# Where the last query transposes are issued: ahead of the gates or between the gates' products

## The chip, the cores and the metric

One core of a Trainium2 chip runs the whole program in one launch. The metric is the device time of an execution in microseconds (us). The engines are TensorE (PE, with its weight loads as PEld), VectorE (DVE), ScalarE (ACT), GpSimd (POOL) and SyncE (SP, whose queue issues the DMAs); each works through a queue of its own in order, and semaphores hold an instruction until its inputs are there.

## What is computed

Two layers of a streaming encoder, for a prompt of 2048 tokens and 8 samples of 16 tokens, D = 1024, all float32. Layer 0 is an RMS norm, one wide projection, and two mixers whose outputs are gated, concatenated and projected back. Layer 1 is a pooled layer that this change doesn't touch.

```python
z = rms_norm(h, norm_g) @ w_in
a_q, a_k, a_v, a_g, b_qkv, b_g, b_beta, b_alpha = split_cols(z, AB_WIDTHS)
q = rms_norm(a_q.reshape(Bn, T, A_HEADS, A_HEAD_DIM), q_norm)
...
o_a = swa_prompt(q, k, v, sinks)             # mixer A: banded attention
o_a = o_a.reshape(Bn, T, A_WIDTH) * jax.nn.silu(a_g)
...
o_b, s_new = gated_delta_rule(bq, bk, bv, beta, g, s0.astype(f32), chunk)   # mixer B
o_b = rms_norm(o_b, o_norm).astype(h.dtype).reshape(Bn, T, B_WIDTH) * jax.nn.silu(b_g)
y = h + jnp.concatenate([o_a, o_b], axis=-1) @ w_out
```

## The kernel before, in words

The tokens are worked through in four groups of four 128-token blocks; group 0 also carries the samples as a fifth block (`GROUPS`, L31). A group runs all of layer 0 and then all of layer 1. Products are made in three passes of float32r (high times high, low times high, high times low): `proj_fm` (L695, products at L702 to L704) makes 128 output columns for up to 512 tokens (two pieces of 320 in group 0) with eight steps of three products; `tok_major` (L1273, products at L1281 to L1283) makes 256 columns for one block of 128 tokens.

Layer 0 treats the heads in two pairs. For each pair: the keys of mixer B (`b_keys`), then its queries and values (`b_queries`), each with a convolution; and the queries of mixer A (`a_queries`, L1359), ahead of `b_queries` for pair 0 and behind it for pair 1. After that come the gates: `gates_early(0)` (L1590), four projections whose results are multiplied at once into pair 0's outputs, and `gates(1)` (L1604), four more.

In `a_queries` each block's product is copied by ACT (L1376), squared by ACT and summed by DVE (`head_norm`, L1295 and L1296), raised to the power -1/2 by POOL (L501) and multiplied by POOL twice (L1304, L1305). Then four PE transposes (L1388; for the sample block two, L1383) bring it into columns; ACT copies them out (L1390) and DVE makes the low half (L1392). This last part is the job `qcols`. A job `end`, behind all blocks, frees two buffers and starts the attention of that pair, `a_attend` (L1425: scores at L1445 and L1446, softmax with DVE at L1449, transposes at L1459, products at L1474 to L1476; in group 0 also the samples' attention with two loads at L1535).

The order of the work is written by a small planner with a clock of its own, which counts estimated us. `tick(us)` is called after every step of products (0.64 for three products of 512 columns, 0.40 for 320, 0.64 for two steps of `tok_major`), advances the clock, issues the pending jobs that are due and lets the running jobs take their next steps. `defer(us, fn)` puts a job into `pend`; `start(gen)` starts a job that takes a step each time the planner's clock passes what its last step yielded; `queue` is worked off by one worker job in order; `drain()` (L396) steps that worker until the queue is empty; `flush()` (L377) issues all that is pending at once, whatever its due time; `finish(job)` (L368) steps a job to its end. The costs that matter here: `DEF` = 7.0 for `qcols` (7.1 for `end`), `ATT` = 2.4, 2.4, 1.2, 1.2 for the steps of an attention unit, `INV` = 0.6 for one of the 31 steps of mixer B's triangular inverse, `VAL` = 1.8 for a value job's wait.

```python
defer(DEF, qcols)            # L1395, for each block
...
def end():
    drop(*zs[0:2])
    st["A", jp] = start(a_attend(jp), 0.6)
defer(DEF + 0.1, end)
```

The planner's order is not the last word. What the program traces is put into the engines' queues by a builder that keeps this order as a priority, but takes an instruction that it reckons ready ahead of an earlier one that it reckons not ready. The trace shows it in places: gate products stand ahead of transposes that the code issues before them.

Mixer B of pair 1 runs beside the gates: `b_inverse` (L979) solves 32x32 blocks on DVE (L995, L996), copies the result (L1000), writes it to DRAM (L1002, L1003) and loads it back in another arrangement (L1011, L1013); PE then joins the blocks, beginning at L1022. The other loads on SP's queue are the weights: in group 0 from the input with a split into high and low (L459, L471, L475), later ready-made (L448), two ahead of use and three buffers in all; and the input rows of the residual (L1640).

Of the kernel before, what the change touches and what calls it, by code (L numbers as in the profile page):

```python
# [237 lines left out]
def hybrid_kernel(  # L238
# [24 lines left out]
    def buf(shape, tag, bufs=2, dt=F32):  # L263
        return sb.tile(shape, dt, tag=tag, name=nm(tag), bufs=bufs)
# [103 lines left out]
    def finish(*js):  # L368
        for j in js:
            while j is not None and j.alive:  # L370
                if j.busy:
                    raise RuntimeError("a job waits for itself")
                j.step()
                if j.wait and j.alive and not progress():
                    raise RuntimeError("jobs wait for each other: " + ", ".join(v[2] for v in held.values()))

    def flush():  # L377
        while pend:
            pend.pop(0)[1]()
# [16 lines left out]
    def drain():  # L396
        while queue or running[0]:
            if work.busy:
                raise RuntimeError("the queue waits for itself")
            work.step()  # L400
# [279 lines left out]
    def group(gix, norm_job):  # L680
# [14 lines left out]
        def proj_fm(w=None, parts=None):  # L695

            wh, wl = w or weight()
            for t0, t1 in parts or pieces:
                pp = psum("pj")
                w = t1 - t0  # L700
                for k in range(KT):
                    mm(pp[:, 0:w], wh[:, k, :], xh[:, k, t0:t1], start=(k == 0), stop=False)  # L702
                    mm(pp[:, 0:w], wh[:, k, :], xl[:, k, t0:t1], start=False, stop=False)  # L703
                    mm(pp[:, 0:w], wl[:, k, :], xh[:, k, t0:t1], start=False, stop=(k == KT - 1))  # L704
                    if k < KT - 1:
                        tick(0.00125 * w)
                yield pp[:, 0:w], t0, t1
                tick(0.00125 * w)
# [3 lines left out]
        def silu2(dst, pp):  # L712

            S.activation(dst, pp, AF.Tanh, scale=0.5)  # L714
            V.scalar_tensor_tensor(dst, dst, 1.0, pp, op0=ALU.add, op1=ALU.mult)  # L715
# [541 lines left out]
        def b_gated(pr, e, gt):  # L1257

            a = st["o", pr][:, e, :]
            for b0, b1 in banks:  # L1260
                po = psum("tp")
                for c in range(b0, b1):
                    T_.transpose(po[:, P * (c - b0):P * (c - b0) + P], a[:, P * c:P * c + P], ident)
                tk = slice(P * b0, P * b1)
                V.scalar_tensor_tensor(a[:, tk], po[:, 0:P * (b1 - b0)], on_h, gt[:, tk],
                                       op0=ALU.mult, op1=ALU.mult)

        def a_gated(jp, j, gt, t0, t1):
            a = st["att", jp][:, j, t0:t1]
            V.scalar_tensor_tensor(a, a, 0.5, gt, op0=ALU.mult, op1=ALU.mult)  # L1270
# [319 lines left out]
        def gates_early(pr):  # L1590

            for e in range(2):
                gt = buf([P, TMAX], "t", NT)
                for pp, t0, t1 in proj_fm():
                    silu2(gt[:, t0:t1], pp)
                    if t1 == n:
                        b_gated(pr, e, gt)
            for j in range(2):
                for pp, t0, t1 in proj_fm():
                    gt = buf([P, 512], "t", NT)  # L1600
                    silu2(gt[:, 0:t1 - t0], pp)
                    a_gated(pr, j, gt[:, 0:t1 - t0], t0, t1)

        def gates(pr):  # L1604
            gs = []
            for _ in range(2):
                gt = slot([P, 2, n])
                for e in range(2):
                    for pp, t0, t1 in proj_fm():
                        silu2(gt[:, e, t0:t1], pp)  # L1610
                gs.append(gt)
            return gs
# [13 lines left out]
                used.extend(u)  # L1626
                yield 1.2

        drain()
        flush()  # L1630
        finish(st["B", 0], st["A", 0])
        gates_early(0)
        ops0, used0, ops1, used1 = [], [], [], []
        gs = gates(1)
        finish(st["B", 1])
# [173 lines left out]
    for gix in range(len(GROUPS)):  # L1809
        norm_job = group(gix, norm_job)  # L1810
# [19 lines left out]
```

## Time and profile before

| | |
|---|---|
| three runs, median (lowest to highest) | 1918.76 us (1918.02 to 1921.17) |
| the profiled execution's own time | 1920.49 us |
| its span, first to last instruction | 1918.6 us |
| busy: PE / PEld / DVE / ACT / POOL | 96% / 83% / 63% / 38% / 26% |
| mean granted TensorE clock | 0.986 of 2.4 GHz |
| DMA | 337.51 MB, mean 176 GB/s |

Busy shares are of the span. A wait is the idle time of an engine just before an instruction, put down to the releaser that came last. All times in rows are us from the span's start unless marked ns. The change concerns four short stretches, one for each group, where the queries of pair 1 end and the gates begin: about 248, 777, 1204 and 1637 us into the span.

### The profile page before, as it was taken

To read this page: it belongs to the slowest core of one execution; us is meant where nothing else is said; L and a number is where in the kernel's file an instruction comes from. 1 tells how busy PE (TensorE), PEld (TensorE's weight loads), DVE (VectorE), ACT (ScalarE), POOL (GpSimd) and SP (SyncE) were. 2 spreads that over 40 slices of the span, in tenths; PEclk is the share of its full clock that TensorE was granted. 3 is DMA by queue.
4 is the path that set the end of the run, shared out by engine and by line. 5 is a ranking of instruction groups with operands and counts; after the bars stand their busy time and mean duration, and the time that the engine had idled before them with its cause. 6 is when DMAs were issued, how large, how long until landed. Compare 5 with 4: busy or idle time off the path is not lost. (4 is left out here: it accounts for less than half of the span.)

```text
span 1918.6 us, 30851 instructions
## 1 busy us (share of the span) xinstructions
PE 1834.6 (96%) x11362; PEld 1601.5 (83%) x11362; DVE 1205.8 (63%) x3215; ACT 722.2 (38%) x1846; POOL 494.6 (26%) x628
## 2 busy tenths in 40 slices
PE   6999989999999999999999999999999999999999
PEld 5988878878997988787888988787888978787887
DVE  6797957555665697754345597664345697754342
ACT  4465336323332474441222474341222474441210
POOL 5633451423332413310012413210012413210000
PEclk9998989999999999999999999999999999999999
DMA  7433453655668533435467533435457533435454
GB/s 274 143 132 125 135 195 96 237 197 205 222 240 297 202 113 121 146 132 186 157 219 287 200 116 100 153 121 187 168 207 292 198 107 111 153 124 187 172 189 189
DMA packets 94578, 337.51 MB, mean 176 GB/s; under 512 B 35884, under 2 KB 44332, under 8 KB 64988
## 3 DMA queue, kind: packets, MB, share of 16 engines
q1 hardware_dynamic: 94428, 335.54, 50.0%
q8 instruction: 90, 1.47, 0.3%
q14 instruction: 60, 0.49, 0.1%
HBM read 256.93 MB, written 78.58 MB: 175 GB/s over the span
## 5 line engine op out<-in xcount | busy, mean ns | idle before, releaser
L702 PE MATMUL pj<-XH,w 128*128 128x512 f32 (+3 forms) x1488 | 544.1, 366 | 5.4 <-ACT cb L852 3.4
L703 PE MATMUL pj<-XL,w 128*128 128x512 f32 (+3 forms) x1488 | 534.1, 359 | 0.1
L704 PE MATMUL pj<-XH,w 128*128 128x512 f32 (+3 forms) x1488 | 533.7, 359 | 0.0
L702 PEld LDWEIGHTS pj<-XH,w 128*128 128x128 f32 x1488 | 284.1, 191 | 34.7 <-ACT cb L852 3.6
L704 PEld LDWEIGHTS pj<-XH,w 128*128 128x128 f32 x1488 | 283.5, 191 | 30.4 <-issue 0.2
L703 PEld LDWEIGHTS pj<-XL,w 128*128 128x128 f32 x1488 | 284.1, 191 | 28.9 <-issue 0.7
L475 POOL TENSOR_TENSOR w<-wst,w 128x640 fp32r<-128x640 f32 (+2 forms) x60 | 106.2, 1770 | 154.6 <-ACT w L471 150.9
L1281 PE MATMUL pj<-w,XH 128*128 128x256 f32 (+1 forms) x368 | 107.2, 292 | 0.3 <-DVE VL L1327 0.3
L1283 PE MATMUL pj<-w,XL 128*128 128x256 f32 (+1 forms) x368 | 104.7, 285 | 0.0
L1282 PE MATMUL pj<-w,XH 128*128 128x256 f32 (+1 forms) x368 | 104.5, 284 | 0.0
L756 DVE TENSOR_TENSOR A<-pj,A 128x512 f32<-128x512 f32 x40 | 27.6, 690 | 106.0 <-PE pj L735 106.0
L471 ACT CAST w<-wst 128x1024 fp32r<-128x1024 f32 (+1 forms) x60 | 61.2, 1020 | 52.5 <-PE sc L735 42.0
L715 DVE SCALAR_TENSOR_TENSOR A<-A,pj 128x512 f32<-128x512 f32 x36 | 24.7, 687 | 88.2 <-ACT A L714 88.2
L735 PE MATMUL rc<-w,B 128*128 128x512 f32 x200 | 78.0, 390 | 0.0
L735 PE MATMUL pj<-w,B 128*128 128x512 f32 x200 | 77.9, 390 | 0.0
L1688 DVE TENSOR_TENSOR B<-cb 128x526 f32<-128x526 f32 x32 | 22.7, 709 | 79.5 <-ACT cb L1733 74.3
L1281 PEld LDWEIGHTS pj<-w,XH 128*128 128x128 f32 x368 | 70.3, 191 | 1.8 <-DVE VL L1327 0.5
L1282 PEld LDWEIGHTS pj<-w,XH 128*128 128x128 f32 x368 | 70.2, 191 | 1.1 <-issue 0.5
L1283 PEld LDWEIGHTS pj<-w,XL 128*128 128x128 f32 x368 | 70.2, 191 | 0.0
L475 DVE TENSOR_TENSOR w<-wst,w 128x384 fp32r<-128x384 f32 (+2 forms) x60 | 49.1, 818 | 32.7 <-ACT w L471 32.6
L733 PE MATMUL rc<-w,B 128*128 128x512 f32 x176 | 69.4, 394 | 0.0
L733 PE MATMUL pj<-w,B 128*128 128x512 f32 x176 | 68.7, 390 | 0.0
(488 smaller groups left out, 4294.8 us busy)
## 6 DMA issues: line engine op xcount, KB each, us to landing
w<-wk SPq DMA_DIRECT2D x168, 1024.0 KB, 4.9
wk<-w SPq DMA_DIRECT2D x56, 1024.0 KB, 6.5
wst<-in_wts SPq DMA_DIRECT2D x56, 512.0 KB, 4.3
A<-in_x SPq DMA_DIRECT2D x22, 512.0 KB, 4.5
w<-wk SPq DMA_DIRECT2D x6, 1056.0 KB, 5.7
B<-in_x SPq DMA_DIRECT2D x12, 512.0 KB, 4.8
w<-wk SPq DMA_DIRECT2D x12, 512.0 KB, 3.2
out_y<-B SPq DMA_DIRECT2D x9, 512.0 KB, 3.4
```

What stands on the lines that cost most here:

```text
L471: S.copy(hi, st)
L475: eng.tensor_tensor(lo[:, a:b], st[:, a:b], f32(hi[:, a:b]), op=ALU.subtract)
L702: mm(pp[:, 0:w], wh[:, k, :], xh[:, k, t0:t1], start=(k == 0), stop=False)
L703: mm(pp[:, 0:w], wh[:, k, :], xl[:, k, t0:t1], start=False, stop=False)
L704: mm(pp[:, 0:w], wl[:, k, :], xh[:, k, t0:t1], start=False, stop=(k == KT - 1))
L715: V.scalar_tensor_tensor(dst, dst, 1.0, pp, op0=ALU.add, op1=ALU.mult)
L733: mm(pp, oh[:, tk], wt[0][:, k, :], start=(kk == k == 0), stop=False)
L735: mm(pp, ol[:, tk], wt[0][:, k, :], start=False, stop=(kk == k == 1))
L756: V.tensor_tensor(ysl, open_.pop(b), ysl, op=ALU.add)
L1281: mm(pp[:, 0:N], xh[:, k, tk], wh[:, k % 4, :], start=(k == 0), stop=False)
L1282: mm(pp[:, 0:N], xh[:, k, tk], wl[:, k % 4, :], start=False, stop=False)
L1283: mm(pp[:, 0:N], xl[:, k, tk], wh[:, k % 4, :], start=False, stop=(k == KT - 1))
```

## The change

`drain()` is removed, and `flush()` goes from ahead of `gates_early(0)` to behind it. The pending `qcols` jobs and `end` are then issued by `tick` when they are due, between the products of the first gates.

```diff
@@ -1626,10 +1626,9 @@
                 used.extend(u)
                 yield 1.2
 
-        drain()
-        flush()
         finish(st["B", 0], st["A", 0])
         gates_early(0)
+        flush()
         ops0, used0, ops1, used1 = [], [], [], []
         gs = gates(1)
         finish(st["B", 1])
```

## Rows read from the trace of the kernel before

**Rows 1.** The page's head and part 1: busy us, share of span, instructions

```profile
span 1918.6 us, 30851 instructions
...
PE 1834.6 (96%) x11362; PEld 1601.5 (83%) x11362; DVE 1205.8 (63%) x3215; ACT 722.2 (38%) x1846; POOL 494.6 (26%) x628
```

**Rows 2.** Waits of PE, whole span: line <- waited for: us total, times, longest

```profile
PE tp L1388 <- POOL B L1305: 17.6, 10, 3.4
```

**Rows 3.** Waits of PE in 250:330, 776:850, 1204:1280, 1636:1712, first entry of each

```profile
PE tp L1388 <- POOL B L1305: 6.5, 4, 3.4
...
PE tp L1388 <- POOL B L1305: 3.2, 2, 2.9
...
PE tp L1388 <- POOL B L1305: 4.4, 3, 3.0
...
PE tp L1388 <- POOL B L1305: 3.4, 1, 3.4
```

**Rows 4.** Timeline of PE, group 2: start, us, engine, line, tiles, count, [idle before <-releaser]

```profile
1204.23 0.28 PE L1283 MATMUL pj<-w,XL 128*128 128x256 f32 x1
...
1208.78 0.66 PE L1388 MATMUL tp<-first,B 128*128 128x128 f32 x4 [2.97 <-POOL B L1305]
...
1212.70 1.11 PE L1388 MATMUL tp<-first,B 128*128 128x128 f32 x4 [0.81 <-POOL B L1305]
...
1214.04 0.63 PE L703 MATMUL pj<-XL,w 128*128 128x512 f32 x1
1214.46 0.63 PE L704 MATMUL pj<-XH,w 128*128 128x512 f32 x1
...
1217.38 0.39 PE L703 MATMUL pj<-XL,w 128*128 128x512 f32 x1
1217.60 0.39 PE L704 MATMUL pj<-XH,w 128*128 128x512 f32 x1
```

**Rows 5.** Windows, groups 1 to 3: us, busy by engine, PEclk, DMA share, GB/s

```profile
770.00:800.00 30.00, 26.31 (x162) 23.08 (x161) 28.01 (x91) 16.18 (x48) 11.17 (x14) 0.94 0.32 117
1200.00:1230.00 30.00, 25.58 (x145) 22.01 (x144) 26.25 (x86) 15.08 (x43) 9.33 (x13) 0.89 0.33 112
1632.00:1660.00 28.00, 24.61 (x137) 21.43 (x136) 25.51 (x82) 13.58 (x40) 8.98 (x12) 0.88 0.31 114
```

**Rows 6.** Timeline of PE, group 1, queries of pair 0: last product, blocks 2, 3

```profile
663.99 0.28 PE L1283 MATMUL pj<-w,XL 128*128 128x256 f32 x1
...
668.72 0.60 PE L1388 MATMUL tp<-first,B 128*128 128x128 f32 x4
...
671.91 0.60 PE L1388 MATMUL tp<-first,B 128*128 128x128 f32 x4
```

**Rows 7.** Timeline of PE, group 0: a gate product, blocks 0 and 3

```profile
250.01 0.31 PE L703 MATMUL pj<-XL,w 128*128 128x320 f32 x1
...
253.04 0.66 PE L1388 MATMUL tp<-first,B 128*128 128x128 f32 x4 [1.12 <-POOL B L1305]
...
263.84 1.12 PE L1388 MATMUL tp<-first,B 128*128 128x128 f32 x4 [0.43 <-POOL B L1305]
```

**Rows 8.** The inverse's way to PE: SP and PE timelines, group 1; landings (L1002, L1011)

```profile
801.12 0.41 SPq L1003 DMA_DIRECT2D Xd<-A  x1
...
805.93 0.34 SPq L448 DMA_DIRECT2D w<-wk  x1
...
807.29 0.60 SPq L1011 DMA_DIRECT2D A<-Xd  x1
...
813.30 0.69 PE L1022 MATMUL sc<-A,B 32*32 32x32 f32 x16
...
DMA to landing us min/median/max: 2.2/2.2/2.2
...
DMA to landing us min/median/max: 5.6/5.6/5.6
```

**Rows 9.** Timeline of DVE, group 3

```profile
1646.95 0.76 DVE L1392 SCALAR_TENSOR_TENSOR A<-tp,gq,A 64x512 fp32r<-64x512 f32 x1 [1.65 <-ACT A L1390]
```

## The prediction

> **What bounds the kernel now.** I read the page's head first. TensorE (PE) is busy for 1834.6 of 1918.6 us, 96% [rows 1]; so a microsecond counts if PE stands still in it or runs at its lower clock. The second view is PE's waits over the whole execution. The largest entry is the one this change is about: the query transposes of L1388 waited 17.6 us, in ten waits, for POOL's multiplication at L1305 [rows 2]. The same view cut to the four stretches in which each group goes over to its gates holds 6.5, 3.2, 4.4 and 3.4 us of it [rows 3], 17.5 together. So all of it sits at the forced issue; the same transposes of the first head pair, which no flush forces, shared the other 0.1.
>
> PE's timeline of group 2 shows how it happens. The last product of the queries starts at 1204.23, the transposes of block 2 start at 1208.78 after 2.97 us of nothing, those of block 3 at 1212.70 [rows 4]. What makes them late is the chain behind a block's product (ACT copy and square, DVE reduction, POOL power and two multiplications), which for block 3 ends 8.35 us after the last product (1212.70 less 1204.23 and some 0.12 for that product's own step). In that time the gates' products, which depend on none of it, stand behind. The third thing to see is the clock: the mean granted clock of the stretches of groups 1 to 3 is 0.94, 0.89 and 0.88 [rows 5]. After the idle time it is at its 1.2 GHz level, and the same product then steps 0.42 us (1214.04 to 1214.46) where it steps 0.22 later (1217.38 to 1217.60) [rows 4].
>
> **The change, part by part.** `drain()` goes first. By the planner's costs its queue is empty there: the last value job ends some 6 planner us after its convolution (3.6 for the conv's rest and the job's own wait, 0.6 more, and what was ahead of it), and the queries that follow take 10.2 (12.8 in group 0). It issues nothing, so removing it costs and gives nothing.
>
> `flush()` moves behind the first four gate projections. A transposition job is put in with a delay of 7.0, blocks follow each other by four ticks of 0.64, so three blocks are pending, due 1.24, 3.80 and 6.36 after the last product, and the end job, which starts the attention of pair 1, at 7.10. With a tick of 0.64 per step of three gate products in groups 1 to 3, they come out after 2, 6, 10 and 12 steps; the moved flush then finds nothing. No instruction is added or dropped. Twelve transposes, three ACT and three DVE copies a group go later on their queues, and so does all that the attention of pair 1 issues, 12 ticks later: scores, softmax and products, in group 0 also POOL's clearing of two small tiles and the cache loads on SP. Those loads come to stand nearer the next weight load, but weights are fetched two ahead, and PE waited for none in the four stretches; I cost that at nothing under this cover.
>
> Where that puts the transposes is not a guess: the first pair's are issued in just this way, among the products of the next convolutions. There blocks 2 and 3 start 4.6 and 7.8 us after the last product (663.99 + 0.12 to 668.72 and 671.91) and wait for nothing [rows 6]. Beside the chains' ends: block 2 of group 2 was ready at 4.4, before 4.6; block 3 at 8.35, which is 0.55 after 7.8. Sum for groups 1 to 3: 3.2 + 4.4 + 3.4 = 11.0 us of idle time removed, less 0.55 each, 1.6, left at block 3.
>
> Clock. Slow time in the three stretches is 2 x (0.06 x 30 + 0.11 x 30 + 0.12 x 28) = 16.9 us [rows 5]. About 2.6 of it are PE's own waits, already counted (0.3 and 0.8 in groups 1 and 2, about 1.5 in group 3). In the other 14.3 a product loses 0.20 of 0.42 us, 48%: 6.9 us come back (1.6, 2.8 and 2.5) if no such wait is left. The Trainium skill ("TensorE: Matmul & The Clock Gate", Terms) prices a throttled stretch at its time times the share of pulses withheld, which would be 8.4 us and make the sum larger by 1.5. I keep the rows' 6.9, because the rule counts time in which PE had nothing to run.
>
> Group 0 I cost apart. There the first transposes stand behind gate products in PE's order (the 17th at 250.01, the transposes at 253.04) [rows 7], although the code issues them ahead: whoever builds the queues had reckoned them not ready and moved them itself. Blocks 0 and 1 aren't even pending at the flush, and block 2, due after 4 steps (a tick is 0.40 here), stands later than that already. Only block 3's 0.43 us [rows 7] is the flush's. Bounds 0 and 6.5 [rows 3]; I take 0.4, because the edit doesn't touch what put the other three there.
>
> What is late next. PE comes to all later work 4.2, 6.6 and 5.3 us sooner in groups 1 to 3 (idle, plus clock, less 0.55). The first thing that doesn't follow PE is the triangular inverse of pair 1: DVE ends it, two transfers write it out (issued until 801.12, landed 2.2 later, 803.3), loads bring it back, and PE's L1022 reads it at 813.30, 0.4 after the third load's landing (807.29 + 5.6) [rows 8]. The loads stood on SP's queue behind a weight load that waited for PE until 805.93 [rows 8]; that one moves with PE, so they can start 3.0 us sooner (803.3 against 805.93 + 0.34) even if the inverse ends no sooner. Then L1022 would wait 4.2 - 0.4 - 3.0 = 0.8 us, and by the same numbers 3.2 and 1.9 in groups 2 and 3: 5.9 as the upper bound. But DVE, 93% busy in group 1's stretch (28.01 of 30) [rows 5], sheds work ahead of the inverse's end, which lies in the midst of the gates: the second attention unit's scores now come at tick 17 in place of 5, and its softmax pieces, some 3 us of DVE by my estimate, go behind. That would clear nearly all; the lower bound is 0. I take 1.4, nearer to 0.
>
> The attention itself has room: by the planner it took 19.8 us of the 41 that eight gate projections cover and will end at 27.5; in group 0 at 46.7 of 51.2. Its PE work is the same and stays among products.
>
> Sum: 11.0 - 1.6 + 6.9 + 0.4 - 1.4 = 15.3 us. The profiled execution took 1920.49 (span 1918.6), which becomes 1905.2; it stands 1.7 above the median of the three runs, 1918.76, which becomes 1903.5. A measurement here can tell 0.2%, 3.8 us, from no change.
>
> **The rivals.**
> Group 0 clears too: if the builder's estimates shift with the new order, its 6.1 us of other waits and some 2.3 of clock (the mean of the other groups) follow: 23.7 in all, 1895. For it: its blocks wait for the same POOL line. Against: their place wasn't the flush's doing [rows 7].
>
> Given back at the inverse: the bound of 5.9 holds in place of 1.4, 10.8 gained, 1908.0; and where waits of 1.9 to 3.2 us drop the clock again, as 2.97 did [rows 4], up to 5.3 more goes, to 1913.3. For it: L1022 stands only 0.4 us behind its data [rows 8]. Against: the work that DVE sheds.
>
> The change doesn't do what it says: the build orders each queue by its own estimates, and might put the transposes of groups 1 to 3 where they were, as it did with group 0's. Then 1918.8. Against: the first pair's it left among the products [rows 6].
>
> Slower: the copies at L1392 hold DVE. DVE works in order; where L1392 stands too early DVE idles for its transposes (1.65 us) [rows 9], the inverse's next step behind it, and now the transposes come later. The Trainium skill ("TensorE: Matmul & The Clock Gate", the table at the head) calls VectorE's queue a strict FIFO; the row agrees. If that adds D to the inverse's end in each group, L1022 waits D longer and the clock falls there again: 15.3 - 4.5 - 6.9 - 3D. From D = 1.3 us the kernel is slower than before; at 3 us it is 5.1 slower, 1923.9. Against: in the row's own group that transposition waited behind a forced one, which goes away.
>
> **How the numbers follow.** Forecast 0.60, group 0 too 0.10, given back 0.15, nothing moves 0.07, slower 0.08. The predicted time is the forecast's, 1903.5. The range runs from 1894 (group 0 too) to 1912 (given back, with most of the clock); it leaves out the nothing and slower cases and the far ends of the other two. Faster by over 0.2%: the first three less 0.01 for the third's far end, 0.84; within it 0.08; slower 0.08.
>
> **What would show it.** In the waits of the changed kernel L1388 <- POOL should be near 6 us in group 0 and under 1 in each other group; the granted clock of the three stretches 0.98 or more; the transposes of blocks 1, 2 and 3 behind 6, 18 and 30 gate products; L1022 with waits of about a microsecond at most. I am wrong if L1388 still waits 2 to 3 us in groups 1 to 3, if L1022 or the gates' products (waiting for DVE's L715) show the time instead, or if group 0's waits vanish.

## The result and the profile after

The changed kernel takes 1906.99 us (median of 4 runs, 1905.85 to 1907.71) where the kernel before, measured beside it, takes 1919.28: 12.3 us less by the medians. The ratio on record is 0.9933, with an interval of 0.992 to 0.9945. The time is 3.5 us above the 1903.5 forecast and inside the range. The profiled execution took 1906.73; its span fell by 13.8 us, where 15.3 were forecast.

The page's head and its part 1 (busy us, share of the span, instructions), beside [rows 1]:

```profile
span 1904.8 us, 30852 instructions
...
PE 1826.1 (96%) x11362; PEld 1596.0 (84%) x11362; DVE 1209.9 (64%) x3215; ACT 721.9 (38%) x1846; POOL 495.6 (26%) x628
```

PE has the same 11362 instructions and is busy 8.5 us less: they ran at a higher clock or were stretched less often. The other 5.3 us of the 13.8 are idle time. The waits of PE over the whole span, beside [rows 2] (line, what it waited for, us in total, times, longest):

```profile
PE tp L1388 <- POOL B L1305: 6.1, 3, 3.4
PE tp L1388 <- DVE A L1392: 5.5, 3, 1.9
...
PE tp L1263 <- DVE A L1392: 2.6, 3, 1.3
...
PE tp L1512 <- DVE kd L1511: 1.0, 1, 1.0
```

The wait for POOL went from 17.6 to 6.1, all of it in group 0 now, as forecast. But two entries are new: transposes that wait for DVE's copy at L1392, 5.5 + 2.6 = 8.1 us. The prediction has no term for them. The windows that answer to [rows 5], at the same distance from the group's last queries to within 0.7 us:

```profile
767.00:797.00 30.00, 27.08 (x162) 23.07 (x161) 27.74 (x69) 9.12 (x21) 10.35 (x15) 1.00 0.39 146
1194.00:1224.00 30.00, 26.88 (x153) 22.72 (x152) 26.66 (x65) 8.41 (x19) 10.35 (x14) 1.00 0.43 153
1620.00:1648.00 28.00, 25.48 (x142) 21.52 (x141) 26.55 (x67) 7.80 (x18) 9.53 (x12) 0.94 0.42 152
```

The clock (third number from the right) is back in groups 1 and 2 (0.94 and 0.89 before), but in group 3 it still fell, to 0.94 (0.88 before).

To put the gain where it belongs, I cut each group from the first query product of pair 1 to the first output product of layer 0, a stretch with the same PE work in every kernel here but one. Groups 0 to 3 of the kernel before, as windows:

```profile
223.20:371.50 148.30, 134.81 (x1064) 122.16 (x1063) 98.82 (x308) 64.55 (x176) 52.30 (x42) 0.97 0.49 166
763.40:858.40 95.00, 90.99 (x633) 78.54 (x632) 64.72 (x202) 44.03 (x122) 25.83 (x30) 0.98 0.41 139
1191.50:1288.70 97.20, 92.46 (x633) 79.61 (x633) 65.05 (x202) 44.06 (x122) 25.46 (x30) 0.96 0.40 136
1624.20:1720.10 95.90, 92.31 (x634) 79.22 (x632) 65.44 (x207) 44.20 (x122) 22.64 (x26) 0.96 0.41 139
```

and of the changed one:

```profile
223.20:369.10 145.90, 133.51 (x1064) 120.78 (x1063) 101.52 (x308) 64.72 (x176) 51.57 (x42) 0.98 0.50 167
761.00:853.00 92.00, 88.85 (x633) 77.18 (x633) 65.06 (x202) 43.84 (x122) 25.99 (x30) 1.00 0.41 142
1186.10:1278.00 91.90, 88.55 (x633) 77.14 (x632) 65.00 (x202) 43.82 (x122) 25.92 (x30) 1.00 0.42 141
1612.50:1706.30 93.80, 91.06 (x634) 78.50 (x633) 67.24 (x207) 44.20 (x122) 23.23 (x26) 0.98 0.43 142
```

Behind the stretch a row has its length, then the busy times of PE, PEld, DVE, ACT and POOL. Groups 0 to 3 are 2.4, 3.0, 5.3 and 2.1 us shorter, 12.8 of the 13.8. In groups 1 to 3 PE is busy 2.1, 3.9 and 1.3 us less, 7.3 together; only the other 3.1 of their 10.4 us are idle time. So the clock gave most of it, and the removed wait little, because a new wait came in its place. PE's timeline of group 1 shows it:

```profile
774.39 0.28 PE L1283 MATMUL pj<-w,XL 128*128 128x256 f32 x1
...
775.90 0.60 PE L1388 MATMUL tp<-first,B 128*128 128x128 f32 x4
...
779.12 0.60 PE L1388 MATMUL tp<-first,B 128*128 128x128 f32 x4
...
781.78 0.66 PE L1263 MATMUL tp<-first,A 128*128 128x128 f32 x4 [0.67 <-DVE A L1392]
...
785.62 0.63 PE L1388 MATMUL tp<-first,B 128*128 128x128 f32 x4 [1.80 <-DVE A L1392]
```

Behind the last query product (774.39) stand six gate products, block 1 (775.90), twelve more, block 2 (779.12), six, a transposition of the gating (L1263), six, and block 3 (785.62): behind 6, 18 and 30 gate products, as forecast, and none waits for POOL. But L1263 and block 3 wait for L1392, which makes neither's input. What they lack is a place to write: all of them write PSUM tiles (the memory that holds PE's results here) of the name `tp`. The kernel has two such tiles and uses them in turn (L251), so a set of transposes waits until the set before the last has been copied out. The copies that empty the tiles, from the timelines of ACT and DVE:

```profile
779.75 0.69 ACT L1390 ACTIVATE A<-tp,gq 128x512 fp32r<-128x512 f32 x1 [2.53 <-PE tp L1388]
...
780.96 0.76 DVE L1392 SCALAR_TENSOR_TENSOR A<-tp,gq,A 64x512 fp32r<-64x512 f32 x1
781.75 0.82 DVE L996 TENSOR_TENSOR A<-A,tm 32x247 f32<-32x247 f32 x1
782.60 0.40 DVE L995 TENSOR_TENSOR tm<-A,A 32x240 f32<-32x240 f32 x1
...
784.71 0.76 DVE L1392 SCALAR_TENSOR_TENSOR A<-tp,gq,A 64x512 fp32r<-64x512 f32 x1
```

ACT had copied block 2 out by 780.44 (779.75 + 0.69). DVE came to its half of the same tile at 784.71, behind block 1's copy and six inverse steps (L995, L996), and let go of it at 785.47. Block 3's transposes start 0.15 later, although their input had been there since 782.30, where POOL's L1305 ended. L1263 starts 0.06 after block 1's copy ends (780.96 + 0.76).

The Trainium skill ("Perfetto Trace Analysis", Optimization Strategy) says that the same gap repeating on the engine that should be saturated can mean that there is no room in SBUF or PSUM for the next tile. The trace agrees: 1.80, 1.8 and 1.9 us, once in each of groups 1 to 3.

### The profile page after: what moved, and what is told of

Same layout as the page of the kernel before. It is cut to its first block, busy times and chain, and to the rows that moved or that the text cites. A ratio compares the mean times of both kernels' runs of the same rounds, so it can differ in the third digit from the quotient of the medians.

```text
span 1904.8 us, 30852 instructions
## 1 busy us (share of the span) xinstructions
PE 1826.1 (96%) x11362; PEld 1596.0 (84%) x11362; DVE 1209.9 (64%) x3215; ACT 721.9 (38%) x1846; POOL 495.6 (26%) x628
## 4 chain that ended last, share of the span: by engine, by line
PE 72%; DVE 17%; issue 3%; POOL 3%; ACT 3%; DMA 2%; SPq 0%; DVEq 0%; POOLq 0%; ACTq 0%
PE pj L702 12%; PE pj L704 12%; PE pj L703 12%; PE pj L735 3%; PE pj L733 3%; PE pj L734 3%; DVE tm L995 2%; PE rc L735 2%; PE rc L733 2%; PE rc L734 2%; DVE A L996 2%; PE pj L1281 2%; PE pj L1282 2%; PE pj L1283 2%; PE tp L1459 1%
## 5 line engine op out<-in xcount | busy, mean ns | idle before, releaser
L735 PE MATMUL rc<-w,B 128*128 128x512 f32 x224 | 87.3, 390 | 0.0
L735 PE MATMUL pj<-w,B 128*128 128x512 f32 x224 | 87.2, 389 | 0.0
L715 DVE SCALAR_TENSOR_TENSOR A<-A,pj 128x512 f32<-128x512 f32 x30 | 20.6, 687 | 85.3 <-ACT A L714 85.3
L995 DVE TENSOR_TENSOR tm<-A,A 40x31 f32<-40x31 f32 (+31 forms) x155 | 62.9, 406 | 6.3 <-DMA A<-Ld 3.9
L872 DVE SCALAR_TENSOR_TENSOR B<-cb,taps,B 128x512 f32<-128x512 f32 x78 | 57.9, 742 | 10.9 <-ACT B L861 10.4
```

What stands on the lines that cost most here:

```text
L735: mm(pp, ol[:, tk], wt[0][:, k, :], start=False, stop=(kk == k == 1))
L995: V.tensor_tensor(t3, bc(Lb[:, j + 1:32, j], w), bcm(Xb[:, j, 0:w], r), op=ALU.mult)
```

## Experiments

Four kernels shared a chip with ten runs of the kernel before (median 1920.38): the tile's release, the attention's start, and for group 0 the undoing and the delay of 3.0. The other four shared one with fifteen (1921.37). Ratios are to the kernel before, as recorded; they can differ by 0.001 from those of the medians.

**The tile's release.** Only the second pair's jobs are changed: ACT makes a second, unrounded copy of the 64 rows that hold the low half, and DVE subtracts from that. DVE has as much to do as in the changed kernel, but no longer reads the tile.

```diff
-                    V.scalar_tensor_tensor(low, pt[64:128], gq8[64:128], f32(low), op0=ALU.mult,
-                                           op1=ALU.subtract)
+                    if jp == 0:
...
+                    full = buf([P, 4, P], "pT", 4).rearrange("p i q -> p (i q)")[64:128]
+                    S.mul(full, pt[64:128], gq8[64:128])
+                    V.tensor_tensor(low, full, f32(low), op=ALU.subtract)
```

> For the second pair's query blocks ACT makes a second, full copy of the transposed block in SBUF, and DVE subtracts from that, so the PSUM tile of the transposes is given back by ACT alone and no longer by DVE's L1392. My theory: the rest of the forecast's gain was lost because the next user of the tile waits for L1392, which stands behind steps of the inverse in DVE's queue. Then PE's waits for L1392 (5.5 + 2.6 us) go, the clock of group 3's stretch goes from 0.94 to 0.99 or more, and the time is 1897 to 1900. Rival: DVE is simply full there, and PE waits for the same DVE work at another line (L1022, or a product behind an attention copy); then L1392's rows go but the time stays at 1905 to 1909. A second rival: block 3 waits for POOL at L1305 instead, some 0.5 us per group; then about 1900 to 1902.

Measured: 1903.61 us (1903.02 to 1903.96), ratio 0.9912 [0.9898, 0.9927]. Every wait for the low half's copy is gone. Groups 1 to 3:

```profile
763.90:854.40 90.50, 88.79 (x634) 77.15 (x633) 65.17 (x202) 46.42 (x126) 27.03 (x30) 1.00 0.43 144
1187.50:1277.80 90.30, 88.88 (x633) 77.07 (x632) 65.16 (x202) 46.42 (x126) 27.12 (x30) 1.00 0.43 144
1612.30:1703.50 91.20, 89.53 (x633) 77.11 (x632) 67.12 (x207) 46.90 (x126) 24.27 (x26) 1.00 0.44 146
```

They are 1.5, 1.6 and 2.6 us shorter than in the changed kernel's first profile (the last by its clock too), and the clock is 1.00 in all three. What is left of their waits (the last group's, all of them):

```profile
PE tp L1263 <- DVE A L1265: 0.7, 1, 0.7
PE sc L1022 <- DMA A<-Xd: 0.4, 1, 0.4
PE tp L1388 <- POOL B L1305: 0.3, 1, 0.3
```

So the cause holds, but the theory promised too much: the next transposition of the gating now waits for the previous one's DVE copy (L1265; 0.9, 0.6 and 0.7 us), and the loads of the inverse (L1022) are only just in time. The second rival's POOL wait is there too, at 0.6 and 0.3 us. The time missed its 1897 to 1900 mostly because of group 0, which was longer here by 2.4 us:

```profile
223.70:372.00 148.30, 134.45 (x1063) 122.22 (x1063) 101.25 (x308) 67.94 (x180) 52.38 (x42) 0.95 0.50 165
```

It has 7.3 us of waits for POOL in place of 6.1, 2.1 at the samples' transposes (L1512 in the other kernels) in place of 1.0, and a clock of 0.95 in place of 0.98. Without these 2.4 us the time would still be some 1901, in the second rival's range. Whether a third `tp` tile would have done as well as ACT's copy was not tried.

**The place of the transposes or the start of the attention.** The three pending `qcols` are forced ahead of the gates, as before; only `end` stays late.

```diff
+        for t in list(pend):
+            if t[1].__name__ == "qcols":
+                pend.remove(t)
+                t[1]()
         finish(st["B", 0], st["A", 0])
         gates_early(0)
         flush()
```

> The three pending transposition jobs are forced ahead of the gates as before the change; only the job that starts the second pair's attention stays late. My theory: the gain is from the transposes' place. Then L1388 waits some 17 us for POOL again, the granted clock in the three stretches is back at 0.88 to 0.95, and the time is 1916 to 1921. Rival: the later start of the attention, which leaves DVE and POOL free behind the last queries, brings the gain; then about 1907 with L1388 under 10 us.

Measured: 1914.66 us (1913.63 to 1917.64), ratio 0.9969 [0.9958, 0.998]. The wait is back:

```profile
PE tp L1388 <- POOL B L1305: 17.3, 9, 3.4
```

but the time is below the 1916 to 1921 that I expected, and far from the rival's 1907. Some 6 us (0.0031 of 1920, the interval allows 4 to 8) come from the later start of the attention alone; the later transposes bring the rest, 7 us by the changed kernel's first ratio (0.9969 less 0.9933) and 8.6 by its second (0.9924, below). Groups 1 to 3:

```profile
761.80:856.10 94.30, 90.34 (x634) 78.46 (x633) 64.84 (x202) 43.71 (x122) 25.79 (x30) 0.98 0.41 138
1189.20:1284.20 95.00, 91.14 (x633) 79.27 (x632) 64.89 (x202) 43.69 (x122) 25.78 (x30) 0.96 0.41 137
1618.70:1713.20 94.50, 90.85 (x634) 78.48 (x633) 66.96 (x207) 44.09 (x122) 22.95 (x26) 0.98 0.43 140
```

Beside the kernel before, PE is busy 0.7, 1.3 and 1.5 us less at nearly the same waits. In this kernel only gate products follow the transposes, in the one before the attention's scores come in between, so the low clock behind the waits may cost less here. But part of it can belong to the execution: the clock of group 3 is 0.98 here and 0.96 before, and the next run shows how far one program varies. Why the later start helps stays open.

**The drain alone.** From the kernel before only `drain()` is taken out.

```diff
-        drain()
         flush()
         finish(st["B", 0], st["A", 0])
```

> The kernel before with only the drain taken out, the forced issue left where it was. My theory: the drain's queue is empty there in every group, so the time is that of the kernel before to within 2 us and L1388 waits 17 to 18 us for POOL. Rival: the drain forced work of the value branch ahead of the gates, which now stands later; then the time differs by 3 us or more from the kernel before, in either direction.

Measured: 1920.07 us (1918.28 to 1923.87), ratio 0.9999 [0.999, 1.0008]; L1388 waits 17.2 us for POOL. PE's trace has the same 11362 products and transposes in the same order as the kernel before: the drain was empty, as the prediction worked out. The run is thus a second profile of the kernel before. Groups 1 to 3:

```profile
764.60:860.80 96.20, 92.44 (x634) 79.75 (x633) 64.97 (x202) 44.20 (x122) 25.34 (x30) 0.96 0.39 137
1194.50:1290.80 96.30, 92.35 (x633) 79.76 (x632) 64.95 (x202) 44.21 (x122) 25.31 (x30) 0.96 0.40 137
1626.60:1723.50 96.90, 92.69 (x634) 79.24 (x633) 65.50 (x207) 44.46 (x122) 22.63 (x26) 0.96 0.40 138
```

Beside the first profile they are 1.2 us longer, 0.9 shorter and 1.0 longer, and PE is busy 1.7 us more in the three together. A difference of that size between two profiles says little.

**Group 0.** First, forced issue in group 0 alone.

```diff
+        if gix == 0:
+            flush()
         finish(st["B", 0], st["A", 0])
```

> Forced issue ahead of the gates is put back in group 0 alone (the changed kernel's time is 1907.0, its span 1904.8). My theory: group 0 holds about 2.4 us of the gain (its way from the front of the group to the output product of layer 0 is that much shorter), so the time rises to about 1909.4, and PE's wait of L1388 for POOL in group 0 goes from 6.1 back to about 6.5 us, with L1512's wait back at about 2.4. Rival: the edit does nothing in group 0, since the builder had moved its transposes behind gate products by itself; then 1906.4 to 1907.6 and the same rows in group 0.

Measured: 1908.53 us (1906.81 to 1910.14), ratio 0.9938 [0.9923, 0.9953], which can't be told from the changed kernel's 0.9933. The rows speak for my theory (L1388 waits 6.9 us, L1512 2.4 again, the group takes 149.4 us), but its clock also fell ahead of the edit's place (0.94 in the 30 us from 223, where the changed kernel has 1.00), so the time does not confirm the 2.4 us.

Second, a longer delay for that group's second pair.

```diff
+            late = 3.0 if gix == 0 and jp else 0.0
...
-                defer(DEF, qcols)
+                defer(DEF + late, qcols)
...
-            defer(DEF + 0.1, end)
+            defer(DEF + late + 0.1, end)
```

> In group 0 alone the second pair's transposition jobs get a delay of 10.0 planner us in place of 7.0, with the attention's start behind them. My theory: the 6.1 us that L1388 still waits for POOL in group 0 are there because POOL's chain is later than 7.0 planner us in that group; 3.0 more clear the waits, and with the slow clock behind them (0.92 in the stretch) the time is 1898 to 1902. Rival: the builder places these transposes by its own estimates whatever the program order; then 1906 to 1908 with the same 6.1 us. A second rival: the attention, which ends 1.5 planner us ahead of the gates' end, runs over it and PE waits there; then 1908 or more.

Measured: 1900.70 us (1899.85 to 1900.94), ratio 0.9896 [0.988, 0.9913]. Group 0 falls from 145.9 to 141.6 us:

```profile
223.10:364.70 141.60, 132.46 (x1063) 122.00 (x1062) 100.12 (x308) 64.84 (x176) 52.07 (x42) 0.96 0.51 174
```

The wait of block 2 (1.59 us in the changed kernel) is gone and L1388 waits 4.5 us, which is blocks 0 and 1 (1.12 and 3.37). The theory had all 6.1 us go. The time came in its range because other waits went as well, 1.5 us at L1237 and 1.0 at L1512. So the planner's delay does move block 2, and the next run moves block 1 too: the forecast was wrong to put all of group 0's other waits on the builder's own order. Group 3, with the same instructions as the changed kernel's, is told of below.

Third, 6.0 in place of 3.0.

> Group 0's delay is 13.0 planner us in place of 10.0, groups 1 to 3 as in the changed kernel. My theory: 4.5 us of waits for POOL and 5.15 us of withheld clock are left in group 0 because its POOL chain is later still; they shrink to under 1.5 us of waits, the group takes 136 to 139 us in place of 141.6, and the time is 1895 to 1899. Rival: the attention of the second pair now ends some 4.5 planner us behind the gates' last product; its tail stands open, group 0 takes 142 or more, and the time is 1901 or more.

Measured: 1902.59 us (1901.94 to 1906.63), ratio 0.9915 [0.99, 0.9929]. L1388's waits for POOL fall to 1.4 us as expected, but new ones stand in group 0:

```profile
PE tp L1263 <- DVE A L1392: 3.2, 1, 3.2
...
PE sc L1217 <- DMA A<-in_state_s: 1.5, 1, 1.5
```

and the stretch behind it, up to layer 1's first output product, takes 198.1 us in place of 195.4, since some of the samples' attention now runs there (1026 of 1064 PE instructions are left in the group). Group 0 and that stretch together take 340.1 us, where they take 336.9 with the delay of 3.0 and 341.3 in the changed kernel. So the rival's figures came: 142 us or more in the group, a time above 1901. But three of the five executions took 1902 and two took 1906, and the profile is of one of the two; and the ratio's interval overlaps that of the shorter delay. That the longer delay is the slower one is likely, not shown.

**The two that helped, together.** Against the kernel with ACT's copy:

```diff
+            late = 3.0 if gix == 0 and jp else 0.0
...
-                    if jp == 0:
+                    if jp == 0 or gix == 0:
...
-                defer(DEF, qcols)
+                defer(DEF + late, qcols)
...
-            defer(DEF + 0.1, end)
+            defer(DEF + late + 0.1, end)
```

> Group 0 with the longer delay of the run e4_group0_later, groups 1 to 3 with the second copy on ACT of the run e2_act_frees_tp, which is left out in group 0. My theory: the two gains lie in different groups and add. From the 1899.0 us of span with the longer delay, 1.5, 1.6 and 0.9 us go in groups 1 to 3 (92.0 to 90.5, 91.9 to 90.3, 92.1 to 91.2): span 1895.0, time 1896 to 1898. Rival: the longer way of group 0 in the run with ACT's copy (148.3 against 145.9) was not ACT's work there but comes with any kernel whose later groups change; then group 0 takes 145 or more again in place of 141.6 and the time is 1900 or more.

Measured: 1895.29 us (1894.60 to 1896.07), ratio 0.9871 [0.9855, 0.9886], the fastest here: 26 us below the kernel before and 10 below the changed one, and a little under the 1896 to 1898 expected. Groups 1 to 3 take 90.5, 90.3 and 91.3 us, to 0.1 the lengths with ACT's copy alone. Group 0:

```profile
222.70:362.60 139.90, 130.72 (x1064) 120.04 (x1063) 100.27 (x308) 64.96 (x176) 52.21 (x42) 0.99 0.52 177
```

So changes in the later groups do not lengthen group 0, and its longer way with ACT's copy is likely that copy's doing. In group 0 PE's order of work is that of the run with the longer delay alone, which took 141.6 at a clock of 0.96; these 1.7 us belong to the execution. The gains add, as far as the runs can tell.

**The changed kernel again.**

> The changed kernel itself, beside the others on one chip, to compare them and to see whether its low clock in group 3 comes back. Theory: the low clock behind a wait of 1.9 us is by the margin of that execution, since a run with the same instructions in group 3 and the same wait (1.93 us) did not have it; then the waits for POOL and L1392 are the same (6.1, 5.5, 2.6) while the clock of the stretch may be 0.94 or 1.00, and the time is 1905 to 1909. Rival: the low clock belongs to this program, and comes at the same place with 1.7 us withheld again.

Measured: 1905.27 us (1904.36 to 1907.45), ratio 0.9924 [0.9911, 0.9936]. L1388's 6.1 and 5.5 us and L1263's 2.6 are there to the tenth; the low clock of group 3 is not: its window of 28 us has a granted clock of 1.00, and the group takes 92.1 us in place of 93.8. The same was so in the run with group 0's longer delay, whose PE timeline of group 3 reads:

```profile
1632.31 0.63 PE L1388 MATMUL tp<-first,B 128*128 128x128 f32 x4 [1.93 <-DVE A L1392]
...
1633.25 0.40 PE L704 MATMUL pj<-XH,w 128*128 128x512 f32 x1
1633.48 0.40 PE L702 MATMUL pj<-XH,w 128*128 128x512 f32 x1
```

and that of the changed kernel's first profile, at the same place:

```profile
1636.51 0.98 PE L1388 MATMUL tp<-first,B 128*128 128x128 f32 x4 [1.91 <-DVE A L1392]
...
1638.14 0.63 PE L704 MATMUL pj<-XH,w 128*128 128x512 f32 x1
1638.57 0.63 PE L702 MATMUL pj<-XH,w 128*128 128x512 f32 x1
```

Products 0.23 us apart in the one, 0.43 in the other, behind the same wait: 1.7 us that belong to the execution and not to the program. The runs with group 0 forced and with its delay of 6.0 have the same order there too, waits of 1.92 and 1.91, a clock of 0.94 over the 28 us, and 93.7 us for the group. So three of five profiles have the low clock and two do not.

## Why the prediction was right, and where not

**The sum** was 15.3 us and the span gave 13.8; the mechanism named (PE stands idle at the forced issue, and its clock falls behind it) is what the rows show. The terms fared unevenly, and that the sum came this near is in part luck. The idle time was put 6.3 us too high; the clock (0.4), the inverse (1.4), group 0 (2.0) and gains outside these stretches (1.0) made up 4.8 of it. Two signs that the forecast named came out badly or only just well. The clock of group 3 was 0.94 in the first profile, where it asked for 0.98 or more. And it called itself wrong if L1388 still waited 2 to 3 us in groups 1 to 3: L1388 waits 1.8, 1.8 and 1.9 there, though for DVE and not for POOL.

**Idle time removed, groups 1 to 3: 9.4 forecast, 3.1 measured.** The step that failed is "11.0 us of idle time removed, less 0.55 each, 1.6, left at block 3". It looked at when a block is ready (POOL's chain) and not at where its transposes write. POOL was no longer late there at all; the tile was. The control I took, the first pair's transposes [rows 6], waits for nothing in a stretch where DVE has room. In the kernel before, as a window (busy times stand in the order PE, PEld, DVE, ACT, POOL; DVE's is 8.79 of 15 us):

```profile
660.00:675.00 15.00, 15.00 (x93) 13.18 (x92) 8.79 (x28) 5.64 (x10) 8.02 (x12) 1.00 0.72 226
```

[rows 5] had the figure that mattered for the second pair, 28.01 us of DVE in 30, and I used it for the inverse's end alone. The first experiment shows that cause: with ACT releasing the tile, all 8.1 us of the two entries go, and 3.1, 3.3 and 2.5 us of waits in the three groups become 1.5, 1.4 and 1.4.

**The clock: 6.9 forecast, 7.3 measured**, and 8.9 in the second execution of the changed kernel, in which nothing was withheld in groups 1 to 3 (busy 88.82, 88.73 and 89.32 us against 90.99, 92.46 and 92.31). Against the second profile of the kernel before (the drain alone) both are 1.7 us more, so the profiles give 7.3 to 10.6 and no single figure. All are above the forecast, so my deduction of 2.6 us of waits from the slow time was probably too much. The Trainium skill's rule ("TensorE: Matmul & The Clock Gate", Terms), slow time times the share withheld, gave 8.4 and stands nearer to the 8.9.

**The attention 12 ticks later: nothing forecast, some 6 us measured** where the transposes stay forced. This part of the edit was costed for its work and its cover, not for what it does around the waits. The rows put most of its gain in groups 1 to 3 (3.5 of 4.3 us) into PE's busy time. How much of it is left in the whole change, where these waits are gone, the runs don't show.

**Given back at the inverse: 1.4 forecast, 0 measured.** No wait at L1022 is in the changed kernel. The argument that DVE sheds work fits the rows: in group 1 its last copy of the inverse (L1000) starts at 795.01, 34.0 us behind the group's first query product (761.0), where it was 36.2 before (799.61 less 763.4). That the loads were close was right too: 0.4 us of wait appear in group 3 of the run with ACT's copy.

**Group 0: 0.4 forecast, 2.4 measured** in the first profile and about the same in the second (145.8 us). The run with the drain alone has 148.4 for the kernel before, so both kernels have it twice. Of it 1.3 are PE's busy time (134.81 to 133.51) and the rest idle time: L1512's wait fell from 2.4 to 1.0 with the later attention, L1388 gave its 0.4, some small waits went, and 1.7 more at L1237 took most of that back. The forecast had counted only what the forced issue itself held up in this group, not the attention behind it. By its time the undoing of group 0 alone can't be told from the changed kernel, so the size rests on the profiles. The four groups' errors, 4.5 too much in groups 1 to 3 and 2.0 too little here, with 1.0 us of the gain outside these stretches, make the 1.5 us by which the sum missed.

**Two readings** of the rows were wrong without changing the sum. All ten waits of [rows 2] lie in the four stretches (4, 2, 3 and 1 in [rows 3]), so the first pair shared none of them. And the landing of 2.2 us in [rows 8] is one of group 2, taken over for group 1.

**The rivals.** Group 0 didn't clear, though the longer delay shows that part of it can. The change did what it says. The slower case, L1392 holding DVE's queue ahead of the inverse, didn't come; its reverse did: the inverse in DVE's queue held L1392, L1392 held the tile, and the tile held PE.

## What to carry to other kernels

When a stalled instruction is moved to where its input is ready, ask next where its output goes: which instruction frees that buffer, on which engine, and what stands ahead of it in that engine's queue. Here two engines read one PSUM tile and the fuller one set its release; a second copy on the emptier one was worth more in three of the four groups than the instruction it cost. A delay that suits one group of a schedule need not suit the next: 3 planner us more shortened group 0 by 4.3 us here, 6 more by 3.9, and then the next stretch grew by 2.7.

## What the runs showed that was not expected

After waits of 1.91, 1.92 and 1.91 us PE's clock fell to its lower level for some products, and after two of 1.93 us in the same order of instructions it did not. The waits of 2.93 to 3.39 us, nine in groups 1 to 3 of three kernels, were all followed by the low clock. A single profile's clock in a short stretch is thus worth 1.7 us either way.

With ACT's copy, DVE's subtraction (L1398 there) reads two operands from SBUF, and a POOL multiplication beside it in group 0 took longer:

```profile
260.54 1.07 POOL L1304 TENSOR_TENSOR B<-B,rsa 128x256 f32<-128x256 f32 x1
...
263.67 0.61 POOL L1304 TENSOR_TENSOR B<-B,rsa 128x256 f32<-128x256 f32 x1
```

```profile
260.45 1.71 DVE L1398 TENSOR_TENSOR A<-pT,A 64x512 fp32r<-64x512 f32 x2
```

The first ran beside the two subtractions (260.45 to 262.16), the second beside nothing of the kind: 1.07 against 0.61 us. The Trainium skill ("GPSIMD Engine Reference", Specifications) says that the two engines share their SBUF interfaces, with contention where a DVE instruction has two SBUF inputs; the rows agree. But the changed kernel has such a case too: its L1305 took 1.20 us (at 260.30) beside DVE's copy at L1000, in place of 0.61. That block's POOL work from L501 to L1305 took 3.69 us with ACT's copy and 2.99 without, so this may account for some 0.7 us of group 0's longer way in that run; that it does is not shown.
